# Transposed attention operands in runs of 32, and query loads on another queue, in a hybrid decoder layer

## The chip, the core and the metric

One core of one Trainium2 chip runs the whole layer, in one launch. The metric is the device time of one execution in microseconds (us). The engines are named as in the profile: PE is TensorE (matmuls) and PEld its weight loads, DVE is VectorE, ACT is ScalarE, POOL is GpSimd, and SP is SyncE, which here only issues transfers.

## The reference, cut to what matters

The input is 256 tokens of width 2048. All arithmetic is float32.

```python
h = rms_norm(x, attn_norm_g)
q, k, v, p = split(h @ w_in)              # each 256 x 1024; q, k, v are 8 heads of 128
q, k = rms_norm(heads(q), q_norm_g), rms_norm(heads(k), k_norm_g)
s = q @ k.T * 128 ** -0.5 + rel_bias[bucket(distance)]    # causal; one block of 256 keys
a = softmax(s) @ v
m = multiscale_pool(p) @ pool_w * pool_scale              # causal means over 2, 4, 8, 16 tokens
x = x + concat(a, m) @ w_out
u = rms_norm(x, ffn_norm_g) @ w_up                        # then a causal convolution of width 3
x = x + (silu(gate) * val) @ w_down                       # d_ff 5632
```

With 256 tokens and blocks of 256 keys there is one block, so attention is plain causal attention over the tokens.

## The kernel before

**Weights.** All weights stream through the core once, as 181 chunks of 128 x 2048 float32 (1 MB each), the tile `raw` (four buffers). ACT rounds a chunk to the matmul's fast format (`wh<-raw`, L121), DVE takes the remainder (`wl<-raw,wh`, L122), both into tiles with three buffers, and PE multiplies three of the four products of the halves. `release` then issues the load of the chunk four further on, so the next `raw` load on SP stands behind a DVE instruction.

**Steps.** The program is a list `steps`; a step is half a chunk of PE work. Steps 0 to 15 make values for the first four heads of k and q, steps 16 to 23 (`tok_block`, `ps_tok`, L178) k of heads 4 to 7, 24 to 31 q of heads 4 to 7, 32 to 47 v, 48 to 63 (`feat_block`, `ps_feat`) the pooling inputs; the output projection and the MLP follow. At the head of every second step u stands the split of chunk u/2 + 2. `after(u, f)` hangs the function f behind step u; functions hung at the same step run in the order in which they were registered. Each engine runs its instructions in the order of the program. `deferred` holds a function back until the head of the next step.

**Attention.** Heads go in two groups b of four. For each of q and k: `raw_heads` copies the projection out (ACT, L349), `head_norm` normalises (ACT square L355, DVE sum L357, a small inverse root by ACT and DVE, DVE product L363), `turn` transposes 32 x 32 blocks on DVE (L369) and `store` writes the result to DRAM through POOL's queue (L374). `land` reads it back with the partitions exchanged, in four transfers of 128 KB (L382), so that the head dimension lies on the partitions: `qT` and `kT`, 128 partitions x 1024. In these tiles the eight columns of one 32-token block and its eight (token half, head) combinations are stored with the combination innermost, so that the tokens of one head lie 8 elements apart. `gains` (L392) scales `kT` in place by the norm gains and the softmax factor.

`scores(h)` runs two float32 matmuls (L402, 128 and 256 columns), each of which the profile shows as two passes, with `qT` as the weights and `kT` as the moving operand, both read with a step of 8 elements. DVE adds the bias tile `T` and takes the row maximum (L407), ACT takes exponentials (L414, deferred), `normalise` divides (L419, L421), and `turn`, `store` and `probs_T` bring the probabilities into `eT` the same way, here with three blocks innermost: `head_out` (L438, L440) reads `eT` with a step of 3 elements as the moving operand and `v` as the weights. `T` holds the bias of four heads, and is loaded per group from `band` in DRAM by four transfers (L293).

**What orders the work.** With `at` = 31 and 45 for the two groups: `gains` at `at - 1`, `scores` of the j-th head of the group at `at + 2j`, `normalise`, `turn` and `store` one step later, `probs_T` at `at + 2j + 4`, `head_out` at `at + 2j + 10 - b`. Norms of k stand at steps 19 and 26, of q at 22 and 33; landings of k at 24 and 40, of q at 27 and 41, both on SP; `T` on POOL at 24 and 38. Transfers take eight completion counters per kind of queue in turn, so a transfer also waits for the one eight issues before it on its kind of queue (`DMAHW0` to `7` for SP, `DMASW0` to `7` for POOL, in the listings below).

Of the kernel before, what the change touches and what calls it, by code (L numbers as in the profile page):

```python
# [23 lines left out]
F32 = mybir.dt.float32  # L24
F32R = mybir.dt.float32r
AF = mybir.ActivationFunctionType
# [3 lines left out]
P = 128  # L30
D = 2048
S = 256
NT = S // P
# [44 lines left out]
def layer(ctx: ExitStack, tc: tile.TileContext, xT, wts, par, rel_d, ident_d, icnt_d, out):  # L78
    nc = tc.nc
# [7 lines left out]
    early = ectx.enter_context(tc.tile_pool(name="early", bufs=1))  # L87
# [4 lines left out]
    def aux(name):  # L92
        return mm.tile([P, 512], F32, name=name, tag="aux", bufs=2)

    def small(name):
        return sm.tile([P, 512], F32, name=name, tag="small")
# [129 lines left out]
    ps = small("ps_start")  # L226
# [58 lines left out]
            nc.gpsimd.tensor_copy(rsb[:, S - n1:S - n0], rel[:, 31 - b:32 - b].to_broadcast([NH, n1 - n0]))  # L285
        nc.gpsimd.dma_start(band, rsb[:, None, :].to_broadcast([NH, 32, L]))

    def bias_tile(h0):
        t = early.tile([P, 4, S], F32, name="T", tag="T")
        for q in range(0, P, 32):  # L290
            src = bass.AP(tensor=band.tensor, offset=band.offset + h0 * 32 * L + P - 1 - q,
                          ap=[[L - 1, 32], [32 * L, 4], [1, S]])
            nc.gpsimd.dma_start(t[q:q + 32], src)  # L293
        return t


# [22 lines left out]
    st = {}  # L319
    qs = keep.tile([P, 1], F32, name="qs")  # L320
# [20 lines left out]
    v = early.tile([P, NT, NH * HD], F32, name="v")  # L341
# [10 lines left out]
    def head_norm(n, name):  # L352

        sq = early.tile([P, NT * 4, HD], F32, name="sq", tag="sq")
        nc.scalar.activation(sq, n, AF.Square)  # L355
        m = early.tile([P, NT * 4], F32, name="m", tag="m")
        nc.vector.tensor_reduce(m, sq, axis=AX.X, op=OP.add)  # L357
        for t in range(NT):
            nc.vector.tensor_scalar(m[:, t * 4:t * 4 + 4], m[:, t * 4:t * 4 + 4], 1.0 / HD,
                                    e1[:, t:t + 1], op0=OP.mult, op1=OP.add)  # L360
        r = early.tile([P, NT * 4], F32, name="hr", tag="hr")
        rsqrt(r, m, NT * 4, early, "h")
        nc.vector.tensor_tensor(n, n, r[:, :, None].to_broadcast([P, NT * 4, HD]), op=OP.mult)  # L363
        return turn(n.rearrange("p n d -> p (n d)"), name, NT * 4)

    def turn(src, name, n):

        x = early.tile([P, 4, 32, n], F32, name=name + "x", tag="hn" if n == 8 else "ex", bufs=3 if n == 8 else 2)
        nc.vector.transpose(x.rearrange("p j b n -> p n j b"), src.rearrange("p (n j b) -> p n j b", j=4, b=32))  # L369
        return x, dram.tile([P, 4 * n * 32], F32, name=name + "d", tag=name + "d")  # L370

    def store(xd, queue):
        x, d = xd
        queue.dma_start(d, x.rearrange("p j b n -> p (j b n)"))  # L374

    def land(dst, xd, n, queue):

        d = xd[1]
        for j in range(4):
            src = bass.AP(tensor=d.tensor, offset=d.offset + j * n * 32,  # L380
                          ap=[[4 * n * 32, 32], [32 * 4 * n * 32, 4], [1, n * 32]])
            queue.dma_start(dst[32 * j:32 * j + 32], src)  # L382

    def head_T(d, name, queue):

        dst = early.tile([P, P, NT * 4], F32, name=name, tag=name)
        land(dst.rearrange("p (i b) n -> p i (b n)", b=32), d, NT * 4, queue)
        return dst

    def gains(b):  # L390
        k = st["kT", b].rearrange("p t n -> p (t n)")
        nc.scalar.activation(k, k, AF.Copy, scale=qs)  # L392

    hst = {}
    HALVES = ((0, slice(0, P)), (1, slice(P, L)))
# [1 line left out]
    def scores(h, qT, kT, T):  # L397

        j = h % 4
        ps = small("ps_s")  # L400
        for t, s in HALVES:
            nc.tensor.matmul(ps[:, s], qT[:, :, 4 * t + j], kT[:, :, j:4 * t + j + 1:4].rearrange("p b t -> p t b"),  # L402
                             start=(t == 0), stop=True, skip_group_check=True)
        e = early.tile([P, L], F32, name="e", tag="e", bufs=3)
        mx = early.tile([P, 4], F32, name="mx", tag="mx", bufs=3)
        for t, s in HALVES:
            nc.vector.tensor_tensor_reduce(e[:, s], ps[:, s], T[:, j, (1 - t) * P:], 1.0, NEG, op0=OP.add, op1=OP.max,  # L407
                                           accum_out=mx[:, t:t + 1])
        nc.vector.tensor_scalar(mx[:, :2], mx[:, :2], -1.0, None, op0=OP.mult)
        hst[h] = e, mx  # L410

        def exps():
            for t, s in HALVES:
                nc.scalar.activation(e[:, s], e[:, s], AF.Exp, bias=mx[:, t:t + 1], accum_out=mx[:, 2 + t:3 + t])  # L414
        deferred.append(exps)

    def normalise(h):
        e, mx = hst[h]
        nc.vector.reciprocal(mx[:, 2:4], mx[:, 2:4])  # L419
        for t, s in HALVES:  # L420
            nc.vector.scalar_tensor_tensor(e[:, s], e[:, s], mx[:, 2 + t:3 + t], rrow[:, :(t + 1) * P],  # L421
                                           op0=OP.mult, op1=OP.mult)

    def probs_turn(h):
        hst[h] = turn(hst[h][0], f"e{h}", 3)

    def probs_T(h):
        d = hst[h]
        eT = early.tile([P, P, 3], F32, name="eT", tag="eT", bufs=3)
        land(eT.rearrange("p (i b) c -> p i (b c)", b=32), d, 3, nc.gpsimd)  # L430
        hst[h] = eT

    def head_out(h):
        eT = hst.pop(h)
        ps = aux("ps_av")
        hs = slice(h * HD, (h + 1) * HD)

        nc.tensor.matmul(ps[:, :S], v[:, 0, hs], eT[:, :, :2].rearrange("p t c -> p c t"),  # L438
                         start=True, stop=False, skip_group_check=True)
        nc.tensor.matmul(ps[:, P:S], v[:, 1, hs], eT[:, :, 2], start=False, stop=True, skip_group_check=True)  # L440
        if "cat" not in st:
            st["cat"] = keep.tile([P, KT, 2, S], F32R, name="cat", tag="c")
        cat = st["cat"]
        nc.scalar.activation(cat[:, h, 0, :], ps[:, :S], AF.Copy)
        nc.vector.tensor_tensor(cat[:, h, 1, :], ps[:, :S], cat[:, h, 0, :].bitcast(F32), op=OP.subtract)
# [91 lines left out]
    def after(u, f):  # L537

        hooks.append((u, f))
# [38 lines left out]
    after(17, stats1)  # L578
    after(15, load_late)
    after(17, bias_rows)  # L580
    after(24, lambda: st.__setitem__(("T", 0), bias_tile(0)))
    for b in range(2):
        at = (31, 45)[b]
        for nm, u0, u1 in (("k", (19, 26)[b], (24, 40)[b]), ("q", (22, 33)[b], (27, 41)[b])):
            after(u0, lambda nm=nm, b=b: (st.__setitem__((nm, b), head_norm(st[nm, b], f"{nm}{b}")),
                                          store(st[nm, b], nc.gpsimd)))
            after(u1, lambda nm=nm, b=b: st.__setitem__(
                (nm + "T", b), head_T(st[nm, b], nm + "T", nc.sync)))
        after(at - 1, lambda b=b: gains(b))
        for j in range(4):  # L590
            h, u = 4 * b + j, at + 2 * j
            after(u, lambda h=h, b=b: scores(h, st["qT", b], st["kT", b], st["T", b]))
            after(u + 1, lambda h=h: (normalise(h), probs_turn(h), store(hst[h], nc.gpsimd)))
            after(u + 4, lambda h=h: probs_T(h))
            after(u + 10 - b, lambda h=h: head_out(h))
        if b == 0:
            after(at + 7, lambda: st.__setitem__(("T", 1), bias_tile(4)))


    late = {}  # L600
# [131 lines left out]
    n = len(steps)  # L732
# [72 lines left out]
```

## Time and profile before

| | us |
|---|---|
| median of 3 runs | 1027.61 (1025.4 to 1028.43) |
| the profiled execution, its own time | 1027.24 |
| its span, first to last instruction | 1025.4 |
| PE busy | 1015.9 |
| DVE busy | 712.2 |
| ACT busy | 510.3 |
| POOL busy | 34.1 |

The 1.84 us between the profiled execution's time and its span lie around the program. The granted TensorE clock averages 0.997 of full speed. Busy time of PE is modelled from pipelined matmuls whose spans overlap; what a piece of PE work takes up is read from the chain of waits in order of time, where the pieces follow one another.

### The profile page before, as it was taken

What the parts mean: (1) busy time and instruction counts of PE and PEld (TensorE: products, weight loads), DVE (VectorE), ACT (ScalarE), POOL (GpSimd) and SP (SyncE); (2) the same over time, 40 slices, a digit from 0 to 9 for tenths busy, and PEclk for the clock granted to TensorE, in tenths of its full rate; (3) what the DMA queues carried; (4) which work ended last, traced back from release to release, by engine and by line L of the source; (5) the groups of instructions that cost most, each with busy time, mean ns of one, the idle gap of its engine ahead of it and who ended that gap; (6) DMA issues with size and microseconds to landing.
All of it is one profiled execution on the core that took longest, in us unless ns stands there. A gap on an engine that the chain in (4) does not pass through costs nothing.

```text
span 1025.4 us, 13829 instructions
## 1 busy us (share of the span) xinstructions
PE 1015.9 (99%) x5730; PEld 887.8 (87%) x5730; DVE 712.2 (69%) x772; ACT 510.3 (50%) x521; POOL 34.1 (3%) x75
## 2 busy tenths in 40 slices
PE   9998999999999999999999999999999999999998
PEld 7887878898888888888888888888888888888888
DVE  6787747876667787777655677777765557777763
ACT  6655344455455555555433545545543345555541
POOL 0101222100000000000000000000000000000000
PEclk9998999999999999999999999999999999999999
DMA  9858585556654555455555555555555555555651
GB/s 341 306 218 269 178 253 195 166 204 236 210 201 175 195 193 212 171 205 205 197 176 203 179 198 198 178 210 187 203 197 191 190 205 169 204 202 169 215 192 42
DMA packets 35599, 206.07 MB, mean 201 GB/s; under 512 B 4728, under 2 KB 8056, under 8 KB 12624
## 3 DMA queue, kind: packets, MB, share of 16 engines
q1 hardware_dynamic: 32848, 198.50, 55.1%
q0 software_dynamic: 2688, 6.69, 2.3%
q8 instruction: 45, 0.74, 0.3%
q14 instruction: 18, 0.15, 0.0%
HBM read 199.01 MB, written 6.16 MB: 200 GB/s over the span
## 4 chain that ended last, share of the span: by engine, by line
PE 92%; DMA 4%; DVE 2%; issue 1%; ACT 0%; SPq 0%; DVEq 0%
PE ps_feat L185 55%; PE ps_feat L187 27%; PE ps_val L168 4%; PE ps_tok L178 3%; DMA raw<-in_wts 3%; PE ps_s L402 1%; DVE wl L122 1%; PE ps_feat L194 1%; DMA qT<-q0d 1%; PE ps_pool L194 1%; DMA qT<-q1d 0%; PE ps_av L438 0%; ACT wh L121 0%; DVE m L357 0%; SPq L111 0%
## 5 line engine op out<-in xcount | busy, mean ns | idle before, releaser
L122 DVE TENSOR_TENSOR wl<-raw,wh 128x2048 fp32r<-128x2048 f32 (+3 forms) x189 | 415.6, 2201 | 185.5 <-ACT wh L121 185.4
L185 PE MATMUL ps_feat<-x2h,wh 128*128 128x512 f32 x1408 | 479.1, 389 | 0.0
L121 ACT ACTIVATE wh<-raw 128x2048 fp32r<-128x2048 f32 (+3 forms) x189 | 348.0, 1842 | 99.9 <-PE ps_feat L185 64.6
L187 PE MATMUL ps_feat<-x2h,wl 128*128 128x256 f32 x1408 | 388.6, 276 | 0.0
L185 PEld LDWEIGHTS ps_feat<-x2h,wh 128*128 128x128 f32 x1408 | 264.3, 188 | 54.9
L187 PEld LDWEIGHTS ps_feat<-x2h,wl 128*128 128x128 f32 x1408 | 264.3, 188 | 0.0
L185 PE MATMUL ps_feat<-hid,wh 128*128 128x512 f32 x680 | 231.3, 389 | 0.0
L187 PE MATMUL ps_feat<-hid,wl 128*128 128x256 f32 x680 | 187.7, 276 | 0.0
L185 PEld LDWEIGHTS ps_feat<-hid,wh 128*128 128x128 f32 x680 | 127.6, 188 | 26.5
L187 PEld LDWEIGHTS ps_feat<-hid,wl 128*128 128x128 f32 x680 | 127.6, 188 | 0.0
L455 ACT ACTIVATE fs<-ps_feat 128x512 f32<-128x512 f32 x75 | 45.2, 602 | 157.2 <-PE ps_feat L187 157.2
L185 PE MATMUL ps_feat<-cat,wh 128*128 128x512 f32 x256 | 87.5, 390 | 0.0
L456 DVE TENSOR_TENSOR fs<-ps_feat,fs 128x512 f32<-128x512 f32 x75 | 51.7, 689 | 49.8 <-ACT fs L455 47.2
L178 PE MATMUL ps_tok<-wh,xh 128*128 128x512 f32 x256 | 84.6, 406 | 0.0
L187 PE MATMUL ps_feat<-cat,wl 128*128 128x256 f32 x256 | 70.7, 276 | 0.0
L178 PEld LDWEIGHTS ps_tok<-wh,xh 128*128 128x128 f32 x256 | 49.3, 192 | 10.8
L185 PEld LDWEIGHTS ps_feat<-cat,wh 128*128 128x128 f32 x256 | 48.0, 188 | 10.2
L703 ACT ACTIVATE hid<-y 128x512 fp32r<-128x512 f32 x22 | 13.9, 632 | 86.2 <-DVE y L702 86.2
L178 PE MATMUL ps_tok<-wl,xh 128*128 128x512 f32 x128 | 50.7, 396 | 0.0
L676 ACT ACTIVATE y<-u,pv 128x256 f32<-128x256 f32 x88 | 47.9, 592 | 5.6 <-DVE u L667 5.6
L187 PEld LDWEIGHTS ps_feat<-cat,wl 128*128 128x128 f32 x256 | 48.1, 188 | 0.0
L185 PE MATMUL ps_feat<-xh,wh 128*128 128x512 f32 x128 | 47.4, 412 | 0.0
(146 smaller groups left out, 679.5 us busy)
## 6 DMA issues: line engine op xcount, KB each, us to landing
raw<-in_wts SPq DMA_DIRECT2D x178, 1024.0 KB, 4.8
raw<-in_wts SPq DMA_DIRECT2D x4, 512.0 KB, 7.5
out<-x SPq DMA_DIRECT2D x7, 256.0 KB, 4.5
xboth<-in_xT SPq DMA_DIRECT2D x6, 256.0 KB, 9.2
T<-band POOLq DMA_DIRECT2D x8, 128.0 KB, 7.7
x<-in_xT SPq DMA_DIRECT2D x1, 1024.0 KB, 8.5
raw<-in_wts SPq DMA_DIRECT2D x3, 256.0 KB, 3.6
x<-in_xT SPq DMA_DIRECT2D x1, 768.0 KB, 6.5
```

Of the source, the lines that this page charges most:

```text
L121: nc.scalar.activation(wh, w, AF.Copy)
L122: nc.vector.tensor_tensor(wl, w, wh.bitcast(F32), op=OP.subtract)
L168: nc.tensor.matmul(ps[b][:, t, :], xh[:, k, a, ts], w[:, ws], start=False, stop=(k == KT - 1 and n == 2), skip_group_check=True)
L178: nc.tensor.matmul(ps[:, t, :], act[:, k0 + k, a, ts], w[:, ws], start=(first and k == 0 and n == 0), stop=(last and k == 1 and n == 2))
L185: nc.tensor.matmul(ps, wh[:, ws], act[:, k, :, :], start=(first and n == 0), stop=False, skip_group_check=True)
L187: nc.tensor.matmul(ps[:, S:], wl[:, ws], act[:, k, 0, :], start=False, stop=(last and n == len(ks) - 1), skip_group_check=True)
L194: nc.tensor.matmul(ps, w[:, ws], act[:, k, a, :], start=(first and n == 0 and i == 0), stop=(last and n == len(ks) - 1 and i == 2))
L402: nc.tensor.matmul(ps[:, s], qT[:, :, 4 * t + j], kT[:, :, j:4 * t + j + 1:4].rearrange("p b t -> p t b"), start=(t == 0), stop=True, skip ...
L455: nc.scalar.activation(dst, ps[:, :, S:], AF.Copy)
L456: nc.vector.tensor_tensor(dst, ps[:, :, :S], dst, op=OP.add)
L676: nc.scalar.activation(y[:, m, :], u[:, m, 2:], AF.Identity, scale=cw[2], bias=col(C_CB + f))
L703: nc.scalar.activation(hid[:, ks, 0, :], y, AF.Copy)
```

## The change

The transposed tiles are laid out with 32 tokens innermost instead of the combination of half and head (n = 8) or of block (n = 3). So DVE writes the transposed blocks in runs of 32 elements, and `scores` and `head_out` read runs of 32 elements. The transfers keep their sizes and their runs of 1024 and 384 bytes.

The gains move from `kT`, in place, to `qT`: ACT copies the landed queries (now a tile from the pool `hn`) with the factor into a second tile, in which one head's 128 tokens lie side by side, so `scores` reads its weights without a step.

The query landings go from SP's queue to POOL's and are hung earlier relative to their use: behind steps 26 and 36 instead of 27 and 41, with the second norm of q at 31 instead of 33. The first landing of k is at 23 instead of 24. The bias tile of the first group is at 23 instead of 24, still on POOL; that of the second group goes from POOL to SP, at step 40 instead of 38. The groups of scores begin at steps 32 and 47 instead of 31 and 45, and `head_out` with them.

```diff
-        x = early.tile([P, 4, 32, n], F32, name=name + "x", tag="hn" if n == 8 else "ex", bufs=3 if n == 8 else 2)
-        nc.vector.transpose(x.rearrange("p j b n -> p n j b"), src.rearrange("p (n j b) -> p n j b", j=4, b=32))
+        x = early.tile([P, 4, n, 32], F32, name=name + "x", tag="hn" if n == 8 else "ex", bufs=3 if n == 8 else 2)
+        nc.vector.transpose(x.rearrange("p j n b -> p n j b"), src.rearrange("p (n j b) -> p n j b", j=4, b=32))
...
-    def head_T(d, name, queue):
-
-        dst = early.tile([P, P, NT * 4], F32, name=name, tag=name)
-        land(dst.rearrange("p (i b) n -> p i (b n)", b=32), d, NT * 4, queue)
+    def head_T(d, name, tag):
+
+        dst = early.tile([P, 4, NT * 4, 32], F32, name=name, tag=tag, bufs=3 if tag == "hn" else 1)
+        land(dst, d, NT * 4, nc.gpsimd if tag == "hn" else nc.sync)
         return dst
 
     def gains(b):
-        k = st["kT", b].rearrange("p t n -> p (t n)")
-        nc.scalar.activation(k, k, AF.Copy, scale=qs)
+        q = early.tile([P, NT * 4, 4, 32], F32, name="qT", tag="qT")
+        nc.scalar.activation(q, st["qT", b].rearrange("p i n b -> p n i b"), AF.Copy, scale=qs)
+        st["qT", b] = q.rearrange("p n i b -> p n (i b)")
...
-            nc.tensor.matmul(ps[:, s], qT[:, :, 4 * t + j], kT[:, :, j:4 * t + j + 1:4].rearrange("p b t -> p t b"),
+            nc.tensor.matmul(ps[:, s], qT[:, 4 * t + j, :], kT[:, :, j:4 * t + j + 1:4, :].rearrange("p i t b -> p t i b"),
...
-        nc.tensor.matmul(ps[:, :S], v[:, 0, hs], eT[:, :, :2].rearrange("p t c -> p c t"),
+        nc.tensor.matmul(ps[:, :S], v[:, 0, hs], eT[:, :, :2, :].rearrange("p i c b -> p c i b"),
...
-        nc.tensor.matmul(ps[:, P:S], v[:, 1, hs], eT[:, :, 2], start=False, stop=True, skip_group_check=True)
+        nc.tensor.matmul(ps[:, P:S], v[:, 1, hs], eT[:, :, 2, :], start=False, stop=True, skip_group_check=True)
...
-    after(24, lambda: st.__setitem__(("T", 0), bias_tile(0)))
+    after(23, lambda: st.__setitem__(("T", 0), bias_tile(0, nc.gpsimd)))
     for b in range(2):
-        at = (31, 45)[b]
-        for nm, u0, u1 in (("k", (19, 26)[b], (24, 40)[b]), ("q", (22, 33)[b], (27, 41)[b])):
+        at = (32, 47)[b]
+        for nm, u0, u1 in (("k", (19, 26)[b], (23, 40)[b]), ("q", (22, 31)[b], (26, 36)[b])):
...
-            after(at + 7, lambda: st.__setitem__(("T", 1), bias_tile(4)))
+            after(at + 8, lambda: st.__setitem__(("T", 1), bias_tile(4, nc.sync)))
```

Three places show what this does to the order. The first is the landing of the first group's operands. SP before, from the load of chunk 17 on (a listing names the counter for which a row waits):

```order
L111 DMA raw<-in_wts 128x2048 [waits DMAHW0_49,DVE_49]
L111 DMA raw<-in_wts 128x2048 [waits DMAHW2_49,DVE_49]
L382 DMA kT<-k0d 32x4x256 [waits DMASW1_49]
L382 DMA kT<-k0d 32x4x256
L382 DMA kT<-k0d 32x4x256 [waits DMAHW1_49]
L382 DMA kT<-k0d 32x4x256
L111 DMA raw<-in_wts 128x2048 [waits DMAHW3_49,DVE_49]
L382 DMA qT<-q0d 32x4x256 [waits DMAHW4_49,DMASW2_49]
L382 DMA qT<-q0d 32x4x256 [waits DMAHW5_49]
L382 DMA qT<-q0d 32x4x256 [waits DMAHW6_49]
L382 DMA qT<-q0d 32x4x256 [waits DMAHW7_49]
L111 DMA raw<-in_wts 128x2048 [waits DMAHW0_49,DVE_49]
```

SP now, from the same load on:

```order
L111 DMA raw<-in_wts 128x2048 [waits DMAHW0_49,DVE_49]
L382 DMA kT<-k0d 32x4x256 [waits DMASW1_49]
L382 DMA kT<-k0d 32x4x256 x2
L382 DMA kT<-k0d 32x4x256 [waits DMAHW1_49]
L111 DMA raw<-in_wts 128x2048 [waits DMAHW2_49,DVE_49]
L111 DMA raw<-in_wts 128x2048 [waits DMAHW3_49,DVE_49]
L111 DMA raw<-in_wts 128x2048 [waits DMAHW4_49,DVE_49]
```

The landing of k now stands ahead of the load of chunk 18, and the four query landings are gone from SP. POOL now:

```order
L374 DMA k0d<-k0x 128x1024
L374 DMA q0d<-q0x 128x1024
L293 DMA T<-band 32x4x256 x4
L382 DMA qT<-q0d 32x4x256 x4
L374 DMA k1d<-k1x 128x1024
L374 DMA q1d<-q1x 128x1024
L374 DMA e0d<-e0x 128x384
L374 DMA e1d<-e1x 128x384
L382 DMA eT<-e0d 32x4x96 x4
L382 DMA qT<-q1d 32x4x256 x4
```

Before, POOL had the same stores without the two landings of `qT`; the first now stands right behind the bias tile, the second behind the first head's probabilities.

The second place is ACT behind step 31, where the projection of q for heads 4 to 7 ends (`q1n`). Before:

```order
L392 ACTIVATE kT<-kT,qs 128x1024
L349 ACTIVATE q1n<-ps_tok 128x1024
L121 ACTIVATE wh<-raw 128x2048
L414 ACTIVATE e,mx<-e,mx 128x128
L414 ACTIVATE e,mx<-e,mx 128x256
L355 ACTIVATE sq<-q1n 128x1024
L301 ACTIVATE rs_s<-m 128x8
L302 ACTIVATE rs_r<-rs_s 128x8
L121 ACTIVATE wh<-raw 128x2048
```

Now:

```order
L349 ACTIVATE q1n<-ps_tok 128x1024
L392 ACTIVATE qT<-qT,qs 128x1024
L355 ACTIVATE sq<-q1n 128x1024
L301 ACTIVATE rs_s<-m 128x8
L302 ACTIVATE rs_r<-rs_s 128x8
L121 ACTIVATE wh<-raw 128x2048
L415 ACTIVATE e,mx<-e,mx 128x128
L415 ACTIVATE e,mx<-e,mx 128x256
L121 ACTIVATE wh<-raw 128x2048
```

The gains follow the copy of `q1n` instead of preceding it, and the second norm of q now stands ahead of the split of chunk 18 (the first `wh` of each list) and of the first head's exponentials. On DVE the same: the sum, the product and the transposition of `q1n` now come ahead of that chunk's `wl` and of the first head's scores.

The third place is SP around step 40, with the second group's operands. Before, from the load of chunk 26 on:

```order
L111 DMA raw<-in_wts 128x2048 [waits DMAHW6_49,DMAHW2_49,DVE_49]
L382 DMA kT<-k1d 32x4x256 [waits DMAHW7_49,DMASW7_49,PE_49]
L382 DMA kT<-k1d 32x4x256 x3
L382 DMA qT<-q1d 32x4x256 [waits DMAHW3_49,DMASW1_49]
L382 DMA qT<-q1d 32x4x256 [waits DMAHW4_49]
L382 DMA qT<-q1d 32x4x256 [waits DMAHW5_49]
L382 DMA qT<-q1d 32x4x256 [waits DMAHW6_49]
L111 DMA raw<-in_wts 128x2048 [waits DMAHW7_49,DVE_49]
```

Now, from the same load on:

```order
L111 DMA raw<-in_wts 128x2048 [waits DMAHW6_49,DVE_49]
L293 DMA T<-band 32x4x256 [waits DMASW5_49,DMASW4_49,DMASW6_49,DMASW3_49,DMASW0_49]
L293 DMA T<-band 32x4x256 x3
L382 DMA kT<-k1d 32x4x256 [waits DMAHW7_49,DMASW3_49,PE_49]
L382 DMA kT<-k1d 32x4x256 [waits DMAHW0_49]
L382 DMA kT<-k1d 32x4x256 [waits DMAHW1_49]
L382 DMA kT<-k1d 32x4x256 [waits DMAHW2_49]
L111 DMA raw<-in_wts 128x2048 [waits DMAHW3_49,DVE_49]
```

Behind the load of chunk 26 there are again eight transfers of 128 KB: the bias tile first and k last, where k came first and q last. The eighth takes the counter of that load, and so waits until it has landed, before as now.

More of the change, by code (lines that the diff above doesn't have):

```diff
@@ L286, in bias_rows, with bias_tile @@
         nc.gpsimd.dma_start(band, rsb[:, None, :].to_broadcast([NH, 32, L]))
-    def bias_tile(h0):
+    def bias_tile(h0, queue):
         t = early.tile([P, 4, S], F32, name="T", tag="T")
@@ L292, in bias_tile @@
                           ap=[[L - 1, 32], [32 * L, 4], [1, S]])
-            nc.gpsimd.dma_start(t[q:q + 32], src)
+            queue.dma_start(t[q:q + 32], src)
         return t
@@ L373, in store @@
         x, d = xd
-        queue.dma_start(d, x.rearrange("p j b n -> p (j b n)"))
+        queue.dma_start(d, x.rearrange("p j n b -> p (j n b)"))
     def land(dst, xd, n, queue):
@@ L381, in land @@
                           ap=[[4 * n * 32, 32], [32 * 4 * n * 32, 4], [1, n * 32]])
-            queue.dma_start(dst[32 * j:32 * j + 32], src)
-    def head_T(d, name, queue):
-        dst = early.tile([P, P, NT * 4], F32, name=name, tag=name)
-        land(dst.rearrange("p (i b) n -> p i (b n)", b=32), d, NT * 4, queue)
+            queue.dma_start(dst[32 * j:32 * j + 32].rearrange("a i n b -> a i (n b)"), src)
+    def head_T(d, name, tag):
+        dst = early.tile([P, 4, NT * 4, 32], F32, name=name, tag=tag, bufs=3 if tag == "hn" else 1)
+        land(dst, d, NT * 4, nc.gpsimd if tag == "hn" else nc.sync)
         return dst
     def gains(b):
-        k = st["kT", b].rearrange("p t n -> p (t n)")
-        nc.scalar.activation(k, k, AF.Copy, scale=qs)
+        q = early.tile([P, NT * 4, 4, 32], F32, name="qT", tag="qT")
+        nc.scalar.activation(q, st["qT", b].rearrange("p i n b -> p n i b"), AF.Copy, scale=qs)
+        st["qT", b] = q.rearrange("p n i b -> p n (i b)")
     hst = {}
@@ L428, in probs_T @@
         d = hst[h]
-        eT = early.tile([P, P, 3], F32, name="eT", tag="eT", bufs=3)
-        land(eT.rearrange("p (i b) c -> p i (b c)", b=32), d, 3, nc.gpsimd)
+        eT = early.tile([P, 4, 3, 32], F32, name="eT", tag="eT", bufs=3)
+        land(eT, d, 3, nc.gpsimd)
         hst[h] = eT
@@ L587, in layer @@
             after(u1, lambda nm=nm, b=b: st.__setitem__(
-                (nm + "T", b), head_T(st[nm, b], nm + "T", nc.sync)))
+                (nm + "T", b), head_T(st[nm, b], nm + "T", "kT" if nm == "k" else "hn")))
         after(at - 1, lambda b=b: gains(b))
```

## The prediction

> **What bounds the kernel now.** I read the page's head first, then PE's waits, a table by stretches around them, and the chain of waits in order of time.
>
> ```profile
> span 1025.4 us, 13829 instructions
> PE 1015.9 (99%) x5730; PEld 887.8 (87%) x5730; DVE 712.2 (69%) x772; ACT 510.3 (50%) x521; POOL 34.1 (3%) x75
> ```
>
> PE is busy almost throughout, so time comes off only where PE's own work gets shorter or where PE waits. The view of PE's waits has two that are not at the start, both for a query landing:
>
> ```profile
> PE ps_s L402 <- DMA qT<-q0d: 3.4, 1, 3.4
> PE ps_s L402 <- DMA qT<-q1d: 1.2, 1, 1.2
> ```
>
> The table by stretches (columns: stretch, its length, busy time of PE, PEld, DVE, ACT, POOL, granted clock, DMA share, GB/s) shows what each leaves behind:
>
> ```profile
> 94.30:97.80 3.50, 0.20 (x1) 0.00 (x0) 0.00 (x0) 2.82 (x2) 0.00 (x0) 0.90 1.07 356
> 97.80:104.00 6.20, 6.15 (x15) 4.93 (x16) 4.26 (x10) 1.94 (x5) 0.00 (x0) 0.51 0.66 252
> 148.30:153.00 4.70, 4.66 (x18) 3.80 (x19) 2.85 (x6) 2.24 (x5) 0.00 (x0) 1.00 0.70 288
> ```
>
> Behind the wait of 3.4 us the clock is half for 6.2 us; behind that of 1.2 us it stays full. The chain, in order of time (start, length, what):
>
> ```profile
> 55.95 0.45 PE ps_row L313 x2
> ...
> 97.85 1.74 PE ps_s L402 x4
> 99.59 7.56 PE ps_tok L178 x24
> 107.16 1.39 PE ps_s L402 x4
> 108.55 5.48 PE ps_tok L178 x24
> ...
> 132.97 10.82 DMA raw<-in_wts
> 143.80 4.30 DMA qT<-q1d
> 148.34 1.74 PE ps_s L402 x4
> ...
> 155.55 0.68 PE ps_av L438 x2
> 156.22 0.35 PE ps_av L440 x2
> ...
> 163.68 1.50 PE ps_s L402 x4
> ```
>
> Two steps of v cost 5.48 us at full clock and 7.56 behind the first wait. At the second group the last landing of q starts only when a weight load of 10.82 us has landed, whose completion counter it takes over.
>
> **The first wait.** It costs 3.4 + (7.56 - 5.48 = 2.1) + (1.74 - 1.39 = 0.3) = 5.8 us. Does it go? These rows place the new landing. The timeline of POOL (start, length, what, and in brackets the idle time before it):
>
> ```profile
> 78.72 0.54 POOL L374 DMA_DIRECT2D q0d<-q0x  x1 [9.78 <-DVE q0x L369]
> 79.26 2.22 POOL L293 DMA_DIRECT2D T<-band  x4
> ```
>
> The timelines of PE and of ACT:
>
> ```profile
> 94.11 0.39 PE L178 MATMUL ps_tok<-wh,xh 128*128 128x512 f32 x1
> ```
>
> ```profile
> 91.61 1.16 ACT L392 ACTIVATE kT<-kT,qs 128x1024 f32<-128x1024 f32 x1 [0.58 <-DMA kT<-k0d]
> 94.54 1.02 ACT L349 ACTIVATE q1n<-ps_tok 128x1024 f32<-128x1024 f32 x1 [1.77 <-PE ps_tok L178]
> ```
>
> The transfers by issue (count, size of one, median us from issue to landing):
>
> ```profile
> raw<-in_wts SPq DMA_DIRECT2D x178, 1024.0 KB, 4.8
> q0d<-q0x POOLq DMA_DIRECT2D x1, 512.0 KB, 2.9
> T<-band POOLq DMA_DIRECT2D x8, 128.0 KB, 7.7
> qT<-q0d SPq DMA_DIRECT2D x4, 128.0 KB, 9.8
> kT<-k1d SPq DMA_DIRECT2D x4, 128.0 KB, 11.2
> ```
>
> The store of q lands at 78.7 + 2.9 = 81.6, as the four issues of `T` end. The four landings follow until 81.6 + 2.2 = 83.8 and no longer queue behind weight loads. With 7.7 to 11.2 us each they are in at 91.5 to 95.0. `kT` leaves SP before the load of chunk 18 instead of behind it, so it comes no later than now. ACT copies `q1n` from 94.5 to 95.5, then does the gains (1.16 in place; I take the same for the copy, which has the same 128 x 1024 elements) to 96.7. PE starts its last matmul of step 31 at 94.11 and, at 5.48 / 24 = 0.23 a matmul, would start step 32 at 94.3 and end it at 94.3 + 5.48 / 2 = 97.1. The scores find their queries with 0.4 us to spare. So the 5.8 us go; bounds: 5.8, and 3.0 if the landing comes some 3 us late without the slow clock.
>
> **The layout on PE.** A head's scores take 1.39 to 1.50 us in the chain (1.43 as a middle), its `head_out` 0.68 + 0.35 = 1.03, each for 384 columns in two passes, 768 column passes: 1.86 ns per pass with a step of 8 elements, 1.34 with a step of 3. `ps_row` is the same float32 form without a step: 0.45 us for 512 passes, 0.88 ns. The step is what differs between the three. Runs of 32 break the row only every 32nd element, so I take the 0.88, that is 0.67 us a head for each: scores 8 x (1.43 - 0.67) = 6.1 us, `head_out` 8 x (1.03 - 0.67) = 2.9. From the other side, if a run costs what a step of 3 costs, scores gain 8 x (1.43 - 1.03) = 3.2 and `head_out` nothing; a loss is excluded, since most neighbours are nearer than in either step now. The weight loads of the queries fall with it, and lie beside matmuls. All of this stands on PE's own path, and PE has no other cover. [...]
>
> **DVE and ACT behind step 31.** DVE's transposition of 1024 elements takes 2.10 us (L369 below), a sum over as many elements read without a step 1.21 (L357). They lie beside PE, so between no gain and 0.9 us each they are worth nothing directly. But the second norm of q now stands ahead of the split of chunk 18, and PE needs that chunk's `wl` at step 36. Rows of the timelines of DVE and of ACT:
>
> ```profile
> 109.34 1.21 DVE L357 TENSOR_REDUCE m<-sq 128x8 f32<-128x1024 f32 x1
> 113.33 2.10 DVE L369 STREAM_TRANSPOSE q1x<-q1n 128x1024 f32<-128x1024 f32 x1
> 115.27 2.29 DVE L122 TENSOR_TENSOR wl<-raw,wh 128x2048 fp32r<-128x2048 f32 x1
> ```
>
> ```profile
> 99.63 0.29 DVE L407 CUSTOM_DVE_ANT_0 e<-ps_s,T 128x128 f32<-128x128 f32 x1 [6.29 <-PE ps_s L402]
> ```
>
> ```profile
> 100.52 0.40 ACT L414 ACTIVATE e<-e,mx 128x128 f32<-128x128 f32 x1 [3.16 <-DVE mx L409]
> 101.41 1.04 ACT L355 ACTIVATE sq<-q1n 128x1024 f32<-128x1024 f32 x1
> 111.34 1.90 ACT L121 ACTIVATE wh<-raw 128x2048 fp32r<-128x2048 f32 x1
> ```
>
> Gains end at 96.7, the square (1.04) at 97.7; from the sum to `wl` stand 115.27 - 109.34 = 5.9 us, so `wl` of chunk 18 runs from 103.6 to 105.9. PE starts step 36 at 94.3 + 2 x 5.48 + 2 x 0.67 = 106.6: 0.7 us to spare. From then on the order is scores on DVE, exponentials, `wh`, `wl`, each waiting for the last: 100.52 - 99.63 + 101.41 - 100.52 = 1.8, plus 1.9, plus 2.3 = 6.0 us a head, against 5.48 + 0.67 = 6.15 on PE. The lag does not grow, until the copy of v (1.0, ACT) stands ahead of chunk 22's split at step 40, where the spare is about 0.7 + 4 x 0.15 - 1.0 = 0.3. I take 0.3 us for small misses; bounds 0 (transpositions at 1.2) and 2.5.
>
> **The second wait.** SP issues chunk 26's load when `wl` of chunk 22 ends: at 133.0 now, then at 105.9 + 4 x 6.0 + 1.0 = 130.9. Behind it come `T`, then `kT`, the fourth of which shares its counter and waits for it. With the same 10.82 + 4.30 it would land at 146.0; but of the 1.5 MB that move beside it now (`T`, `kT`, `qT`) 1.0 stays, so the weight load should come nearer to the median of 4.8. PE reaches the scores of head 4 at 94.3 + 8 x 5.48 + 4 x 0.67 + 3 x 0.67 = 142.8. So the wait lies between 0 and 3.2 us, against 1.2 + 0.2 (1.74 less 1.50) now. I take 0.7, a gain of 0.7.
>
> POOL gets eight issues more and four fewer, at 2.22 / 4 = 0.55 us each. The second query landing puts 2.2 us in front of the probabilities of head 1 and later heads. Their `head_out` stands six steps (16 us) behind their landing in the program, of which DVE's lag, 105.9 against 97.8 for head 0, takes 8; the other 8 cover the 2.2, so I cost it at nothing, and a probability landing some 6 us slower than now would make PE wait.
>
> **The sum.** The profiled execution took 1027.2 (span 1025.4 and 1.8 around it), 0.4 under the median of the three runs. 1027.2 - 5.8 - 9.0 + 0.3 - 0.7 = 1012.0.
>
> **Rivals.** (1) The layout gains only the lower bound: 3.2 instead of 9.0, which gives 1017.8. For it: no row shows a run of 32. Against: 1.86, 1.34 and 0.88 ns order by step. (2) The second wait grows and takes the slow clock: 3.2 us of wait, and 2.4 for the slow steps as behind the first, instead of 0.7, give 1016.9. For it: the fourth `kT` still waits for a weight load. Against: the load starts 2 us sooner with less beside it. [...] (3) Slower than before: the query landings on POOL come so late that ACT stands still at the gains. `q1n`'s norm, chunk 18's split and PE stand behind that instruction, so each us past 96 is a us of PE, plus 2.4 for the clock. It outweighs the gain of 15.2 only past 108.8, 25 us after the last issue, and at 113 gives 1031; the slowest landing row has 11.2.
>
> **How the numbers follow.** Forecast 0.70, (1) 0.13, (2) 0.11, (3) 0.02, and 0.04 for no net change by several of these. The forecast's own bounds are 1010.4 (no second wait, no misses by DVE, scores at 1.50 now) and 1014.7 (misses of 2.5, a wait of 1.2); the three runs scatter by 1.5 to either side, which sets the low end at 1008.9. The range goes to 1018 to take in (1) and (2). 0.3% (3.1 us) is about what a measurement of this kernel can tell; all cases but (3) and the last are faster by more: faster 0.94, same 0.04, slower 0.02.
>
> **What would show it.** In the changed profile: scores and `head_out` near 0.67 us a head in the chain; no PE wait and a clock of 1.00 at 94 to 104 us; transpositions near 1.2; a wait of at most 2 us for `kT<-k1d` near 143, and chunks' `wl` just ahead of PE from 106 to 131. It is wrong if scores stay above 1 us, or if PE waits for `wl` at each of those chunks.

## The result, and the profile after

The changed kernel takes 1010.74 us (median of four runs, 1010.64 to 1011.13) against 1027.2 for the kernel before on the same chip (1025.4 to 1028.43). The ratio is 0.984, with a 95% interval of 0.9825 to 0.9859: 16.5 us faster. The forecast was 1012.0. The profiled execution took 1010.76, with a span of 1009.0.

The page's head:

```profile
span 1009.0 us, 13833 instructions
PE 1004.1 (100%) x5730; PEld 882.0 (87%) x5730; DVE 708.4 (70%) x772; ACT 509.7 (51%) x521; POOL 39.1 (4%) x79
```

The span is 16.4 us shorter. PE has 11.8 us less busy time (1015.9 before), with the same 5730 instructions; the remaining 4.6 us are waits of PE that are gone. PE's waits, of which these two are all that the view lists:

```profile
PE ps_start L228 <- DVE ones L225: 1.1, 1, 1.1
PE ps_val L168 <- DVE wl L122: 0.2, 1, 0.2
```

Both lie at the start, and both were there before. The view lists no wait of PE for a landing of queries or keys any more. The table by stretches, in the places shown for the kernel before (stretch, length, busy time of PE, PEld, DVE, ACT, POOL, granted clock, DMA share, GB/s):

```profile
94.30:97.80 3.50, 3.50 (x18) 2.97 (x17) 0.51 (x1) 2.96 (x3) 0.00 (x0) 1.00 0.91 346
97.80:104.00 6.20, 6.20 (x30) 5.17 (x29) 5.51 (x9) 2.23 (x3) 0.55 (x1) 1.00 0.03 11
```

PE is busy all through both, at full clock, where it stood for 3.4 us and then ran at 0.51. The chain in order of time (start, length, what):

```profile
55.66 0.43 PE ps_row L313 x2
56.09 40.85 PE ps_tok L178 x180
96.94 0.66 PE ps_s L403 x4
97.60 5.49 PE ps_tok L178 x24
...
126.96 0.43 PE ps_av L439 x2
127.61 5.49 PE ps_tok L178 x24
...
142.68 0.86 PE ps_s L403 x4
...
199.31 2.83 PE ps_pool L194 x24
```

And the row that ends attention in the chain of the kernel before:

```profile
215.98 2.83 PE ps_pool L194 x24
```

From `ps_row` to the first `ps_pool` the kernel before took 215.98 - 55.95 = 160.0 us, this one 199.31 - 55.66 = 143.65. The 16.4 us between them are the whole difference of the spans. It divides into the two waits (3.4 + 1.2), the steps of v behind the first at half clock (7.56 - 5.48 = 2.1), the scores (eight pieces of 1.39 to 1.74, 12.1 in all, against seven of 0.66 and one of 0.86, 5.5: 6.6), and `head_out` (8 x 1.03 against 8 x 0.65: 0.43 for L439, and 0.22 for L441, from its end at 127.39 to the next row at 127.61; 3.0 in all). That makes 16.3.

### The profile page after: what moved, and what is told of

Same layout as the page of the kernel before. It is cut to its first block, busy times and chain, and to the rows that moved or that the text cites. A ratio compares the mean times of both kernels' runs of the same rounds, so it can differ in the third digit from the quotient of the medians.

```text
span 1009.0 us, 13833 instructions
## 1 busy us (share of the span) xinstructions
PE 1004.1 (100%) x5730; PEld 882.0 (87%) x5730; DVE 708.4 (70%) x772; ACT 509.7 (51%) x521; POOL 39.1 (4%) x79
## 4 chain that ended last, share of the span: by engine, by line
PE 99%; DMA 0%; SPq 0%; DVE 0%; ACT 0%; issue 0%
PE ps_feat L185 56%; PE ps_feat L187 28%; PE ps_tok L178 9%; PE ps_val L168 4%; PE ps_feat L194 1%; PE ps_pool L194 1%; PE ps_s L403 1%; DMA raw<-in_wts 0%; PE ps_av L439 0%; PE ps_av L441 0%; SPq L111 0%; PE ps_row L313 0%; SPq L215 0%; DVE wl L122 0%; ACT wh L121 0%; DVE x L713 0%
## 5 line engine op out<-in xcount | busy, mean ns | idle before, releaser
L178 PE MATMUL ps_tok<-wh,xh 128*128 128x512 f32 x256 | 81.7, 395 | 0.0
```

Source lines behind the costliest of these rows:

```text
L178: nc.tensor.matmul(ps[:, t, :], act[:, k0 + k, a, ts], w[:, ws], start=(first and k == 0 and n == 0), stop=(last and k == 1 and n == 2))
```

## The experiments

The time of each is given with its ratio to the kernel before on its own chip, since that kernel's median differs by chip (1024.7 to 1027.2). Edits are told relative to the changed kernel.

### The layout without the schedule

```diff
-        land(dst, d, NT * 4, nc.gpsimd if tag == "hn" else nc.sync)
+        land(dst, d, NT * 4, nc.sync)
...
-        at = (32, 47)[b]
-        for nm, u0, u1 in (("k", (19, 26)[b], (23, 40)[b]), ("q", (22, 31)[b], (26, 36)[b])):
+        at = (31, 45)[b]
+        for nm, u0, u1 in (("k", (19, 26)[b], (24, 40)[b]), ("q", (22, 33)[b], (27, 41)[b])):
...
```

The two bias loads also go back to where they were, both on POOL.

> Only the layout changes (runs of 32, and the queries copied with the gains); queues, landings and steps are those of before. Theory 1 (PE's own work and its waits are two separate terms, but the waits answer to PE): scores and head_out take 0.66 us a head each, 9.0 us less PE work, and the transpositions 1.25 us. The first wait shrinks only by the faster transpositions and gets the copy of q behind its landing, some 2.9 us; the second grows to some 3 us, because PE comes to it sooner than the landing moves. About 1019 us, between 1017 and 1021.5. Theory 2 (the layout is the whole of the change, the schedule does nothing): 1011, with both waits gone. Theory 3 (the gain is in the queues and steps): 1025 to 1027.

1019.51 us (1018.26 to 1019.94), ratio 0.9932 (0.9917 to 0.9947), as theory 1 had it. PE's waits:

```profile
PE ps_s L403 <- DMA raw<-in_wts: 2.9, 1, 2.9
PE ps_s L403 <- ACT qT L392: 2.6, 1, 2.6
```

The chain around them:

```profile
87.24 8.53 DMA qT<-q0d
95.87 1.16 ACT qT L392
97.07 1.65 PE ps_s L403 x4
98.71 6.12 PE ps_tok L178 x24
...
144.58 1.65 PE ps_s L403 x4
146.23 6.21 PE ps_tok L178 x24
```

And the stretches behind the two waits:

```profile
97.80:104.00 6.20, 6.20 (x25) 4.97 (x24) 4.51 (x10) 3.78 (x7) 0.18 (x1) 0.83 0.28 89
146.00:153.00 7.00, 7.00 (x30) 5.74 (x29) 4.42 (x10) 2.11 (x6) 0.56 (x1) 0.88 0.48 164
```

The first row names a weight load, but scores don't read `raw`. PE and its weight loads together stood three times, 8.7 us in all, until ACT's copy of the queries released this line; the 2.6 us of the second row are one of the three. SP issued the second group's queries from 131.11 to 139.32. So the first row too is read here as a wait for queries.

The 9 us of layout were there, but 1.5 of them were given back. Between `ps_row` and `ps_pool` this kernel took 152.3 us (208.23 less 55.92), 8.7 more than the changed one: waits of 2.6 + 2.9, two heads' scores at 1.65 instead of 0.66 and 0.86 (1.8), and two pairs of steps of v at 6.12 and 6.21 instead of 5.49 (1.4). The stalls of the kernel before cost 7.2 in that stretch, as the next kernel shows. With shorter matmuls PE arrives at the second group sooner and waits longer there (2.9 against 1.2), and the reduced clock, which in the kernel before followed only the first wait (0.51, against 1.00 behind the second), now follows both (0.83 and 0.88). At the first group the copy by ACT (1.16) stands between the landing and PE.

### The schedule without the layout

```diff
-        x = early.tile([P, 4, n, 32], F32, name=name + "x", tag="hn" if n == 8 else "ex", bufs=3 if n == 8 else 2)
+        x = early.tile([P, 4, 32, n], F32, name=name + "x", tag="hn" if n == 8 else "ex", bufs=3 if n == 8 else 2)
...
-            nc.tensor.matmul(ps[:, s], qT[:, 4 * t + j, :], kT[:, :, j:4 * t + j + 1:4, :].rearrange("p i t b -> p t i b"),
+            nc.tensor.matmul(ps[:, s], qT[:, :, 4 * t + j], kT[:, :, j:4 * t + j + 1:4].rearrange("p b t -> p t b"),
...
```

> Queues, landings and steps as changed, and the gains in a copy of q, but the old layout with steps of 8 and 3 elements. Theory 1: both waits on landings and the slow clock go (5.8 and 1.4 us), scores stay at 1.4 us and head_out at 1.03, transpositions at 2.1: 1020.0 us, between 1019 and 1021.5. With the slower transpositions chunk 18's remainder is still ready before PE needs it, since PE is slower too. Theory 2 (layout alone matters): 1027. Theory 3 (without the faster transpositions DVE and ACT run late behind step 31): PE waits for the remainders of chunks 18 to 22, 2 us or more, 1022 or above.

1020.17 us (1019.81 to 1020.95), ratio 0.994 (0.9923 to 0.9956), as theory 1 had it. PE has no wait for scores; the chain shows their old price:

```profile
97.95 1.39 PE ps_s L403 x4
...
130.84 0.68 PE ps_av L439 x2
...
155.65 1.50 PE ps_s L403 x4
...
209.48 2.83 PE ps_pool L194 x24
```

From `ps_row` at 56.66 to `ps_pool` it took 152.8 us, 7.2 less than the kernel before. That is the two waits, the half clock behind the first, and what the waits put on the scores right behind them (0.35 and 0.24): 4.6 + 2.1 + 0.6 = 7.3. The new order costs nothing that shows beside this.

### The queries landed on SP

```diff
-        land(dst, d, NT * 4, nc.gpsimd if tag == "hn" else nc.sync)
+        land(dst, d, NT * 4, nc.sync)
```

> The changed kernel with the query landings back on SP's queue, at the new steps 26 and 36. Theory 1 (what matters is where the landing stands in the order, not which queue carries it): the first landing is issued near 83 us behind the load of chunk 19 and lands near 94 to 96, at worst 1 us of wait; 1010.7 to 1012. Theory 2 (the queue with the weight loads is itself too slow): the landing comes 3 us or more too late, the clock halves again, 1014 to 1017.

1011.22 us (1011.01 to 1011.48), ratio 0.9854 (0.9839 to 0.9868), and no wait for scores. On this schedule the queue makes no measurable difference: from `ps_row` to the first scores it took 41.28 us (97.49 less 56.21), as in the changed kernel (96.94 less 55.66), where the first query landing on POOL took 7.2 to 9.4 us from issue. That leaves the place in the order, behind fewer weight loads and more steps ahead of use. Of its parts only the steps of the scores were tried by themselves (next); the earlier steps of the landings and of the second norm, and the moves of the bias tiles, were not.

### The scores at their old steps

```diff
-        at = (32, 47)[b]
+        at = (31, 45)[b]
```

> The changed kernel with the two groups of scores back at steps 31 and 45 (head_out and the second bias tile with them); landings and queues as changed. Theory 1 (the earlier landings remove the waits, the later scores add nothing): at most 0.5 us of wait at the first group and none at the second, since ACT's split of chunk 22 and so the load ahead of k come sooner too; 1010.7 to 1012. Theory 2 (the later scores are what hides the landings): waits of 1 us at the first and 2 to 5 us at the second group, 1013 to 1018.

1012.24 us, ratio 0.9866 (0.9846 to 0.9885), with four runs from 1010.46 to 1014.92. The changed kernel's four runs lie within 0.5 us. In the profiled run, of 1011.9, PE waited for the second landing of k:

```profile
PE ps_s L403 <- DMA kT<-k1d: 0.3, 1, 0.3
```

This kernel reaches the changed one's time in some runs and not in others. To see whether that scatter was the kernel's, three kernels were run together on one chip: the changed kernel again, the same edit again, and the edit `at = (31, 47)`, which moves only the first group.

> The changed kernel once more, unchanged, beside the next two on one chip: 1010.6 to 1011.2 us, as in its first runs.

> The version with the scores back at steps 31 and 45 once more, with more runs. The first time it took 1010.46 to 1014.92, and its profile showed a PE wait of 0.3 us for the second landing of k. Theory 1 (later scores are margin only: the operands land near the moment of use, sometimes after it): median 1011 to 1012.5, and again a scatter of 2 us or more to the slow side. Theory 2 (the one run of 1014.92 was a disturbance of that chip, later scores are worth nothing): within 0.5 us of the changed kernel, all of them.

> Only the first group's scores back at step 31; the second stays at 47. Which group needs the margin? Theory 1a (the second, whose k landing ended the wait in the profile with both early): within 0.5 us of the changed kernel and as narrow. Theory 1b (the first, whose first head took 0.90 us in that profile instead of 0.66, the gains coming after the copy of the projection): the scatter of the version with both early stays, 1011 to 1014. Theory 2: same as the changed kernel.

| scores at | runs | median | lowest | highest | ratio (95%) |
|---|---|---|---|---|---|
| 32 and 47 | 5 | 1011.04 | 1010.6 | 1011.35 | 0.9854 (0.984 to 0.9868) |
| 31 and 47 | 4 | 1011.7 | 1010.73 | 1012.56 | 0.9861 (0.9845 to 0.9876) |
| 31 and 45 | 5 | 1012.1 | 1010.78 | 1016.82 | 0.9873 (0.9852 to 0.9895) |

The lowest runs agree within 0.2 us; what grows is the tail. The ratios' intervals overlap, so the median alone would settle nothing; but the version with both early scattered by 4.5 us on one chip and by 6.0 on another, the changed kernel by 0.5 and 0.75. The run of 1016.82 has a mean clock of 0.998, its neighbours 1.000, which fits a long wait with a reduced clock behind it; only the fastest of the five was profiled, so that stays a reading. With only the first group early, the profile caught a wait in the act:

```profile
PE ps_s L403 <- ACT qT L392: 0.7, 1, 0.7
```

Its chain:

```profile
83.98 9.80 DMA qT<-q0d
...
93.94 1.16 ACT qT L392
95.15 0.92 PE ps_s L403 x4
```

So the later steps look like a margin: they don't shorten the kernel's best runs, they keep it from standing when a landing takes long. With both groups early theory 1 held (a median of 1011 to 1012.5 and a scatter of 2 us or more). Neither 1a nor 1b held alone: with one group early the scatter (1.8 us) lies between, so both groups seem to use their margin, though four runs are few for that.

### The queries' weights with a step of 8

Only the queries go back to the old layout (transposition and copy; the lines below show the copy); keys and probabilities stay in runs.

```diff
-        q = early.tile([P, NT * 4, 4, 32], F32, name="qT", tag="qT")
-        nc.scalar.activation(q, st["qT", b].rearrange("p i n b -> p n i b"), AF.Copy, scale=qs)
-        st["qT", b] = q.rearrange("p n i b -> p n (i b)")
+        q = early.tile([P, P, NT * 4], F32, name="qT", tag="qT")
+        nc.scalar.activation(q.rearrange("p t n -> p (t n)"), st["qT", b].rearrange("p i n b -> p (i n b)"), AF.Copy, scale=qs)
+        st["qT", b] = q
...
```

> The changed kernel with the queries alone in the old layout, so that their weight loads read with a step of 8 elements, while the moving operands keep runs of 32. Theory 1, as the prediction had it (weight loads lie beside matmuls): the loads take 0.33 us instead of 0.19, the scores stay near 0.66 us a head, 1010.7 to 1011.7. Theory 2 (a load that is longer than the matmul beside it sets the pace): four loads of 0.33 make 1.0 to 1.3 us a head, 3 to 5 us in all, 1013.5 to 1016.

1013.0 us (1012.94 to 1013.03), ratio 0.9884 (0.987 to 0.99). The chain's first and last scores:

```profile
96.97 0.94 PE ps_s L407 x4
...
164.10 1.05 PE ps_s L407 x4
```

The weight loads of scores, in this kernel and then in the changed one (count, shortest, median and longest in ns, first and last start):

```profile
L407 PEld LDWEIGHTS ps_s<-kT,qT x32: 315/334/338, 96.6 to 164.5; 128*128 128x128 f32 x32
```

```profile
L403 PEld LDWEIGHTS ps_s<-kT,qT x32: 187/190/193, 96.5 to 162.4; 128*128 128x128 f32 x32
```

The time lies between the two theories; it reads as theory 2 at a smaller price. A head costs 0.94 to 1.06 instead of 0.66: 7.9 us for the eight, against 5.5 in the changed kernel, with no wait of PE in either. From `ps_row` to `ps_pool` this kernel takes 145.8 us (201.49 less 55.69), 2.2 more than the changed one. At the probe's price (next) a plain pass of 128 columns takes 0.11 us, where a weight load here takes 0.33 us and in the changed kernel 0.19; that the longer load sets the pace is a reading of these numbers. So the copy into a plain layout is worth about 2 us, but only once the moving operand is fast: with both operands in steps of 8 the probe shows the price of the moving operand alone (5.57 us for twelve passes against 5.52).

### The price of a step, by itself

Two kernels put groups of six 256-column matmuls behind the last step. In the first all groups stood in one line of code, and the profile gave them one row, so only the starts of some weight loads could be read from it.

> The changed kernel with 18 groups of six matmuls of 256 columns added at its end, on data that are there, with results that nobody reads: float32 with a moving step of 1, 2, 3, 4, 8 and 16 elements, runs of 2, 4 and 8 elements that start 16 apart, weights with a step of 2, 4 and 8; then the fast format with a step of 1, 2, 4 and 8 and runs of 2 and 4. [...] Theory 2 (the cost grows with the step): 2 between 0.88 and 1.34, 4 between 1.34 and 1.86, 16 above 1.86, and runs of 2 dearer than runs of 8.

In the second each group has its own line.

```diff
+    for _ in range(6): nc.tensor.matmul(pr, f[:, :P], f[:, :1 * S:1], start=True, stop=True, skip_group_check=True)
+    for _ in range(6): nc.tensor.matmul(pr, f[:, :P], f[:, :2 * S:2], start=True, stop=True, skip_group_check=True)
...
```

> The program of after with 20 groups of six 256-column matmuls behind its last step, each group on a line of its own, so that the pace of each can be read apart (the numbers they give are not used by the outputs). Float32, moving operand in steps of 1, 2, 3, 4, 8 and 16 elements, then in runs of 2, 4 and 8 elements whose starts lie 16 apart; then weights in steps of 2, 3, 4 and 8 with a plain moving operand; then both in steps of 8; then the fast format in steps of 1, 2, 4 and 8 and in runs of 2 and 4. In an earlier run with these on one line the weight loads started every 0.451 us in step 4, 0.460 us in step 8 and 0.431 us in step 16. [...] Weights: if a load with step 8 sets the pace when the matmul is plain, as in the kernel with stepped weights (0.94 us a head of four passes), 0.24 to 0.31 us a pass for weights in steps of 4 and 8, and about 0.23 for step 2; both in steps of 8 as in the kernel before, 0.46. Theory 2 (cost grows with the step): step 16 above step 8, runs of 2 like step 8. [...]

Its chain, at a granted clock of 1.00: L752 to L757 are float32 with a moving step of 1, 2, 3, 4, 8 and 16, L758 to L760 runs of 2, 4 and 8, L761 to L764 weight steps of 2, 3, 4 and 8, L765 both in 8; L766 to L769 the fast format with a step of 1, 2, 4 and 8, L770 and L771 with runs of 2 and 4. Float32 has 12 passes a group, the fast format 6.

```profile
1005.42 2.59 PE ps_probe L752 x12
1008.01 2.72 PE ps_probe L753 x12
1010.73 4.08 PE ps_probe L754 x12
1014.81 5.41 PE ps_probe L755 x12
1020.22 5.52 PE ps_probe L756 x12
1025.74 5.17 PE ps_probe L757 x12
1030.92 2.61 PE ps_probe L758 x12
...
1046.68 2.86 PE ps_probe L764 x12
1049.54 5.57 PE ps_probe L765 x12
1055.10 0.72 PE ps_probe L766 x6
1055.82 1.36 PE ps_probe L767 x6
1057.19 1.40 PE ps_probe L768 x6
1058.58 1.31 PE ps_probe L769 x6
1059.89 1.33 PE ps_probe L770 x6
1061.22 0.72 PE ps_probe L771 x6
```

Per column and pass (a group's time by 256 columns and its passes), float32 takes 0.84 ns plain, 0.89 with a step of 2, 1.33 with 3, 1.76 with 4, 1.80 with 8 and 1.68 with 16; runs of 2 already cost 0.85. The cost rises up to a step of 4 and, at 8 and 16, no further to speak of, so theory 2 is out. The 1.33 and 1.80 are close to the 1.34 of `head_out` and the 1.86 of scores in the kernel before. With weights in steps of 8 plain 256-column passes take 0.238 us each instead of 0.216; four at that pace make 0.95 us a head, the 0.94 that the kernel with stepped weights showed.

## Why the prediction was right, point by point

**The first wait** (5.8 us). All of it went. The gains ended sooner than forecast. ACT's timeline:

```profile
95.17 1.14 ACT L392 ACTIVATE qT<-qT,qs 128x1024 f32<-128x1024 f32 x1
```

That is 96.3 against the 96.7 worked out. PE's first weight load of scores starts at 96.5 and its scores at 96.94, so 0.2 to 0.6 us were to spare. The landings took a median of 9.0 us from issue, inside the 7.7 to 11.2 assumed, and what the gains followed was the copy of `q1n`. Still it was near: with the scores a step earlier, a landing of 9.8 us cost 0.7 us of wait.

**The layout on PE** (9.0 us). Seven heads of scores took 0.66 us, as forecast (0.67), and one 0.86 (see the second wait); `head_out` 0.43 + 0.22 = 0.65. On the new schedule the layout is worth 9.2 us (152.8 less 143.65). Rival 1, a run at the price of a step of 3, is out: the probe gives runs of 2, 4 and 8 the plain price (2.61, 2.59 and 2.59 us a group, plain 2.59, 4.08 with a step of 3). That runs of 32 cost what the row without a step costs was the author's estimate, since the trace before has no runs; the seven heads at 0.66 us bear it out. What the probe shows for float32 doesn't carry over to the fast format: there a step of 2 and runs of 2 cost 0.89 and 0.87 ns against 0.47 plain, about as much as steps of 4 and 8 (0.91 and 0.85), and only runs of 4 cost the plain 0.47.

**The weight loads** ("lie beside matmuls", worth nothing). This step failed. It holds with the old matmuls (5.57 us against 5.52 in the probe, as above); with the new ones, a head took 0.94 to 1.06 us with loads in the old layout (0.33 us each) and 0.66 with plain ones (0.19). It did no harm to the sum, because the plain pass of 0.88 ns, taken for scores as a whole, supposed plain loads too. A forecast for the run layout with the queries left in steps of 8 would have been wrong by about 2 us.

**DVE and ACT behind step 31** (0.3 us lost). Nothing was lost. DVE's timeline:

```profile
101.29 1.25 DVE L369 STREAM_TRANSPOSE q1x<-q1n 128x1024 f32<-128x1024 f32 x1
102.46 2.25 DVE L122 TENSOR_TENSOR wl<-raw,wh 128x2048 fp32r<-128x2048 f32 x1
```

The transposition took 1.25 instead of 2.10 and the gains ended 0.4 sooner, so `wl` of chunk 18 ended at 104.7, not 105.9, and PE came to it at 106.5: it had 1.8 us to spare instead of 0.7.

**The second wait** (a gain of 0.7). PE's wait of 1.2 us went, but with only 0.3 us to spare. SP's timeline of the landings, and the one row of the waits that names these scores, for PE's weight loads:

```profile
130.01 2.23 SPq L293 DMA_DIRECT2D T<-band  x4
132.36 3.23 SPq L382 DMA_DIRECT2D kT<-k1d  x4
```

```profile
PEld ps_s L403 <- issue: 0.4, 1, 0.4
```

The load of chunk 26 went out at 129.5 (forecast 130.9) and took 5.8 us, not 10.82. The fourth landing of k still waited for it, went out at 135.3 and took 7.1 us, not the 4.30 assumed. So k was in at 142.4, and PE began the scores at 142.68 (forecast 142.8). The weight load had stood 0.4 us and this head took 0.86 us instead of 0.66; whether k's landing caused that, the profile doesn't say. In the second profile of the same kernel the scores began at 143.24 and took 0.66. The mechanism was forecast rightly, but that the landing came just in time is in part luck: the load took less than feared, the landing more. Rival 2, a wait of 3.2 us, did not come true here, but something near it did with the layout alone: the second wait grew to 2.9 us, and the clock was 0.88 in the 7 us behind it.

**The difference.** The forecast is 1.3 us above the median: about 0.5 for the second wait (1.2 + 0.2 gone, 0.2 still paid), 0.3 for DVE and 0.2 for the layout (9.2 instead of 9.0); the rest is rounding and scatter. This execution reached `ps_row` 0.3 us sooner (55.66 against 55.95), but took as much longer behind the first `ps_pool` (809.7 against 809.4), so that adds nothing. Rival 3 found nothing to stand on: the queries on POOL were in at 92.7 us, before PE's scores at 96.94, and moving them to SP changed nothing measurable (ratio 0.9854 against 0.984).

## What to carry to other kernels

Where PE is the bound, read a matmul's price per column from the chain and compare it with a plain matmul of the same format; here a step between neighbours raised it to about double (0.84 to 1.80 ns in float32, 0.47 to 0.91 in the fast format), and runs of 4 elements had the plain price in both formats (2.59 and 0.72 us a group). Speeding up PE's work moves its arrival forward, so a wait that was small can come back larger (1.2 us before, 2.9 with the layout alone): here, between `ps_row` and `ps_pool`, the layout alone took off 7.7 us, the schedule alone 7.2, and both together 16.4. On these few runs, a landing that is just in time showed more in the scatter (4.5 and 6.0 us against 0.5 and 0.75) than in the median. A landing can be just in time without any wait in the view (k was in at 142.4, its scores began at 142.68): compare when it lands with when its reader starts.

## What the runs showed that was not expected

- The granted clock fell to 0.83 and 0.88 over the 6 to 7 us behind waits of 2.6 and 2.9 us, and not behind 1.2. In the kernel before it stood at 0.51 behind 3.4 us, so here the fall went with shorter waits too. The first head's scores behind each took 1.65 us instead of 0.66.
- The first scores of a group took some 0.2 us longer not only behind a short wait of PE (0.92 us behind 0.7, against 0.66) but also where only PE's weight loads had stood for 0.4 us (0.86 in the changed kernel, 0.90 with the scores at their old steps).
- DVE's transposition of 128 x 1024 is also sensitive to the layout of what it writes: 1.25 us in runs of 32 elements against 2.10 where neighbours lie 8 apart. It wasn't on the path before, and became part of the margin at chunk 18.
- In the fast format a step of 2 costs as much as one of 8 (1.36 and 1.31 us for six passes, plain 0.72); in float32 a step of 2 costs nearly nothing (2.72 us for twelve, plain 2.59).
